# RWKV's chunked recurrence on TensorE: small products of one array shape in whole bursts, one PSUM bank for each chunk's output

## The chip, the cores and the metric

One core of one Trainium2 chip runs the whole program: TensorE (PE, with its weight loads as PEld), VectorE (DVE), ScalarE (ACT), GpSimd (POOL), SyncE (SP) and 16 DMA engines. The metric is the device time in microseconds of one execution, the median of several runs; lower is better.

## The reference

Two transformer blocks over 256 tokens of width 2048, all in float32. In the first, differential attention and an RWKV7 mixer work on the same normalised input, are gated, added and projected, and a feed-forward network follows. The second block holds stick-breaking attention, a state-space layer, sparse attention, cross attention and a convolutional feed-forward network; the change leaves it alone. What matters is the recurrence of RWKV7, 32 heads of 64 channels, one token at a time:

```
def _rwkv7_step(state, inp):
    r_t, w_t, k_t, v_t, a_t, b_t = inp
    sa = jnp.einsum('bhij,bhj->bhi', state, a_t)
    state = (state * w_t[:, :, None, :] + sa[..., None] * b_t[:, :, None, :]
             + v_t[..., None] * k_t[:, :, None, :])
    y = jnp.einsum('bhij,bhj->bhi', state, r_t)
    return state, y
```

## The kernel before, in words

**Weight products.** Most of the time goes to products with weights of 512 KB pieces. SP loads a piece, ScalarE rounds it to the high part WH (L163), VectorE subtracts to get the low part WL (L164), and TensorE multiplies three ways (L146 to L148, or in the transposed form L210, L211, L213). Such a product is a generator; each step issues a few matmuls and yields. A step is a tick.

**Lanes.** Everything else runs beside them as generators in lanes (`spawn`, `tick`), which yield the number of ticks to wait. While a lane must be finished before work can go on, `drain` ticks it and calls `fill`, which takes steps of weight products that are not urgent (the gate projections). The order of the emission gives each instruction a priority. A scheduler, working with its own estimate of times, then puts each engine's instructions into a fixed order: of those whose inputs it takes to be ready, the one emitted first. TensorE executes in that order, and a matmul that has to wait holds up all behind it.

**RWKV in chunks** (`rwkv`, L373). The 32 heads are four groups of eight: four tiles j of 128 channels, two heads o each on partition halves 0 to 63 and 64 to 127. The 256 tokens are four chunks c of 64. For each group:
- `rkv` (L469): the projections r, k, v of the group, 24 weight pieces;
- `rw_prep` (L505): decay factors, scaled operands AR and BK, in `s3` the bonus (L590) and the scores S (L597: for each half o, four chunks into one PSUM bank), transposed copies;
- `rw_chain` (L640): the inverse of a triangular 64x64 matrix of each head and chunk. VectorE inverts 32x32 diagonal blocks in 31 steps beside the next group's `rkv`; the results go through DRAM (dT, dX) to the tiles T1 and Xs. Two groups of 32x32 products (L701, L712) make the off-diagonal block, each evacuated by ScalarE in two halves (L705, L716);
- the recurrence itself (L721 to L766), chunk by chunk. Each chunk has five groups of 8 small matmuls, one for each (j, o): L727 (state into U, not in chunk 0), evacuated by two VectorE additions (L730); L736 (inverse times U), evacuated half by VectorE (L738), half by ScalarE (L739); L746 (next state, not in chunk 3), then L751 and L752 on VectorE; and for the output Y, in one loop over (j, o), L761 (state times AR, not in chunk 0) and L762 (UV times S) accumulate into the same piece of PSUM. L763 copies the output to Y. After most groups the generator yields 2 ticks;
- `rw_norm` (L768): group norm, bonus and gate, beside the preparation of the next group.

An f32 matmul shows up as two instructions in the trace. PSUM has eight banks of 512 f32 columns: four (`pm`) for weight products, four (`ps`) for all small products, taken and given back in turn.

The output loop before:

```
for j in range(4):
    for o in range(2):
        q = 64 * o
        out = ps[q:q + 64, j * 64:j * 64 + 64]
        if c:
            nc.tensor.matmul(out, St[q:q + 64, j], AR[q:q + 64, j, c, 1, :], start=True, stop=False)
        nc.tensor.matmul(out, UV[:, j, c, o], S[:, o, j, c, 64:128], start=(c == 0), stop=True)
```

Of the kernel before, what the change touches and what calls it, by code (L numbers as in the profile page):

```python
# [10 lines left out]
F32 = mybir.dt.float32  # L11
F32R = mybir.dt.float32r
AF = mybir.ActivationFunctionType
ALU = mybir.AluOpType
# [28 lines left out]
class K:  # L43
# [29 lines left out]
    # Side work runs in lanes: generators that yield the number of ticks to wait. A tick is one step of a  # L73
    # weight product (six matmuls), so that what a lane emits next on TensorE finds its operands ready.
# [83 lines left out]
    def split(self, w, p, WH, WL):  # L158
        """hi/lo of a pair of weight tiles"""
# [60 lines left out]
    def proj(self, w, nb, xa, dst, scale=1.0):  # L220
        """dst [128 channels, 4, T] = scale * (X @ W[:, 512 columns]).T"""
# [12 lines left out]
    def ln_exp(self):  # L234
        """loads the one table set that has both functions"""
        return self.nc.scalar.preload_act_table_set("natural_log_exp_and_others")

    def after(self, a, b):
        """a is scheduled after b"""
        self.tc.add_manual_dep(a.ins, b.ins.name, mybir.DependencyInfo(mybir.DependencyClass.NoSync, mybir.DependencyReason.DATA), reason="order")  # L240

    def to_hl(self, src, n, H, L, g=None, k0=0):
        """H/L[:, k0+kt, :] = hi/lo of (src(half, kt) transposed) * g[:, kt]."""
# [19 lines left out]
    def hl_both(self, pool, n=NKT):  # L263
        """room for a pair; hi and lo of a column tile are neighbours"""
# [6 lines left out]
    def rstd_of(self, ss, n, eps):  # L271
        """(ss / n + eps) ** -0.5 into a new [128, m] tile."""
# [6 lines left out]
    def rsqrt(self, r):  # L279
        """r <- r ** -0.5: a first guess from the exponent bits and three Newton steps"""  # L280
# [18 lines left out]
    # ---------------------------------------------------------------- program  # L299
# [35 lines left out]
    def x_in(self, xp):  # L335
        """the input, its transpose as hi/lo pair, and 1 / rms"""
# [168 lines left out]
    def rw_prep(self, g):  # L505
# [5 lines left out]
        # per-group LoRA weights  # L511
# [24 lines left out]
        # squared key norms (their maximum with the guard), inverted  # L536
# [20 lines left out]
            # a  # L557
# [5 lines left out]
            # k' = k * (1 + (a - 1) * k_a)  # L563
# [8 lines left out]
        def s2(j):  # L572
# [3 lines left out]
            # scaled operands  # L576
# [9 lines left out]
        def s3(j):  # L586
            # bonus
# [52 lines left out]
    def rw_chain(self, g):  # L640
        nc, rc, re = self.nc, self.rc, self.re
        AR, BKt, UV, S, G, bon, LB = self.rwg
        # inverses of the 32x32 diagonal blocks of I - A_ab (transposed), one block per partition
# [41 lines left out]
        for o in range(2):  # L685
            D_(T1[64 * o:64 * o + 32].rearrange("s j c t -> s (j c) t"), dT[o * 32:o * 32 + 16].rearrange("u s t -> s u t"))
# [7 lines left out]
        # off-diagonal block of the inverse  # L694
        Ms = re.tile([128, 16, 32], F32, tag="T1", name=self.nm("Ms"))
        ps = self.pst()
        for j in range(4):
            for c in range(4):
                for o in range(2):
                    q, u = 64 * o, 4 * j + c  # L700
                    nc.tensor.matmul(ps[q + 32:q + 64, u * 32:u * 32 + 32], S[q:q + 32, o, j, c, 32:64], T1[q:q + 32, j, c],  # L701
                                     start=True, stop=True, tile_position=(q, q + 32))
        for o in range(2):
            q = 64 * o
            nc.scalar.activation(Ms[q + 32:q + 64], ps[q + 32:q + 64].rearrange("p (u t) -> p u t", u=16), AF.Copy)  # L705
        yield 2
        ps = self.pst()
        for j in range(4):
            for c in range(4):
                for o in range(2):  # L710
                    q, u = 64 * o, 4 * j + c
                    nc.tensor.matmul(ps[q:q + 32, u * 32:u * 32 + 32], Ms[q + 32:q + 64, u], Xs[q + 32:q + 64, j, c, 32:64],  # L712
                                     start=True, stop=True, tile_position=(q + 32, q))
        for o in range(2):
            q = 64 * o
            nc.scalar.activation(Xs[q:q + 32, :, :, 32:64], ps[q:q + 32].rearrange("p (j c t) -> p j c t", j=4, c=4), AF.Copy)  # L716
# [3 lines left out]
        St = None  # L720
        for c in range(4):  # L721
            if c:
                ps = self.pst()
                for j in range(4):
                    for o in range(2):
                        q = 64 * o
                        nc.tensor.matmul(ps[q:q + 64, j * 64:j * 64 + 64], AR[q:q + 64, j, c, 0, :], St[q:q + 64, j], start=True, stop=True)  # L727
                for o in range(2):
                    u = UV[64 * o:64 * o + 64, :, c, o, :]
                    nc.vector.tensor_tensor(u, ps[64 * o:64 * o + 64, :256].rearrange("p (j t) -> p j t", j=4), u, op=ALU.add)  # L730
                yield 2
            ps = self.pst()
            for j in range(4):
                for o in range(2):
                    q = 64 * o
                    nc.tensor.matmul(ps[q:q + 64, j * 64:j * 64 + 64], Xs[q:q + 64, j, c], UV[q:q + 64, j, c, o], start=True, stop=True)  # L736
            pu = ps[:, :256].rearrange("p (j t) -> p j t", j=4)
            nc.vector.tensor_copy(UV[0:64, :, c, 0, :], pu[0:64])  # L738
            nc.scalar.activation(UV[64:128, :, c, 1, :], pu[64:128], AF.Copy)  # L739
            yield 2  # L740
            if c < 3:
                ps = self.pst()
                for j in range(4):
                    for o in range(2):
                        q = 64 * o
                        nc.tensor.matmul(ps[q:q + 64, j * 64:j * 64 + 64], BKt[:, j, c, q:q + 64], UV[:, j, c, o], start=True, stop=True)  # L746
# [3 lines left out]
                if c:  # L750
                    nc.vector.tensor_tensor(Sn, pn, St, op=ALU.add)  # L751
                    nc.vector.tensor_tensor(Sn, Sn, gb, op=ALU.mult)  # L752
                else:
                    nc.vector.tensor_tensor(Sn, pn, gb, op=ALU.mult)
            ps = self.pst()
            for j in range(4):
# [1556 lines left out]
```

## Time and profile before

| | |
|---|---|
| median of 3 runs | 3492.47 us (3492.26 to 3493.1) |
| span of the profiled execution | 3503.7 us |
| TensorE busy | 3365.8 us, 96% of the span |
| weight loads busy | 2784.5 us, 79% |
| VectorE, ScalarE, GpSimd busy | 2273.7, 1710.8, 684.8 us |
| RWKV stage, preparation of group 0 to recurrence of group 3 | about 130 to 795 us of the span |

The profile comes from an execution of its own; for it only the span is known. Times in the rows are from the start of that span. Busy time of TensorE counts an instruction from its start to its modelled end, so instructions overlap and a sum of durations is more than the time that passes; distances between starts are the safer measure. PEclk is the granted clock as a share of 2.4 GHz; it has two levels, 1.0 and 0.5, and a stretch shows the mean.

### The profile page before, as it was taken

The page shows a single profiled execution, that of the slowest core. Times are in us where ns is not written, and L with a number is a line of the kernel's source. Part 1 is how long each engine was busy: PE and PEld are TensorE (multiplying, and loading weights), DVE is VectorE, ACT ScalarE, POOL GpSimd, SP SyncE. Part 2 cuts the span into 40 slices and gives each one's busy share as a digit, 9 for nine tenths or more (in the row PEclk, how much of TensorE's full clock was granted, in tenths as well). Part 3 has the DMA queues.
Part 4 walks back from the last instruction along what each step waited for, and adds up shares of the span by engine and source line. Part 5 has one row for each costly group of instructions (what it writes and reads, how often), then busy time and mean ns, then how long its engine had stood idle before and what let it go on. Part 6 is the DMA issues. An engine that isn't in the chain of part 4 may idle for free.

```text
span 3503.7 us, 50392 instructions
## 1 busy us (share of the span) xinstructions
PE 3365.8 (96%) x18954; PEld 2784.5 (79%) x18954; DVE 2273.7 (65%) x3636; ACT 1710.8 (49%) x2675; POOL 684.8 (20%) x882
## 2 busy tenths in 40 slices
PE   8999999999999999999999999779999999999998
PEld 7877777778788888888888887557677788888886
DVE  5676675755766766554555565986777766566566
ACT  5544453534445555444443444336545554455453
POOL 0203021321211210210110101950103311011011
PEclk9999998989999999999999999979999999999999
DMA  6553534446656774666666665335456466666665
GB/s 213 154 169 98 150 107 126 127 137 190 202 180 185 263 246 151 189 187 192 186 187 193 187 202 186 115 106 175 135 169 203 144 188 188 191 187 189 190 186 156
DMA packets 177765, 607.04 MB, mean 173 GB/s; under 512 B 22427, under 2 KB 27372, under 8 KB 176752
## 3 DMA queue, kind: packets, MB, share of 16 engines
q1 hardware_dynamic: 168800, 580.25, 53.8%
q0 software_dynamic: 7856, 21.94, 2.0%
q8 instruction: 149, 2.44, 0.3%
q10 hardware_dynamic: 864, 1.62, 0.1%
q14 instruction: 96, 0.79, 0.1%
HBM read 584.29 MB, written 22.59 MB: 173 GB/s over the span
## 4 chain that ended last, share of the span: by engine, by line
PE 75%; DVE 8%; issue 6%; DMA 4%; ACT 2%; POOL 1%; DVEq 0%; ACTq 0%; POOLq 0%; SPq 0%
PE pm L211 26%; PE pm L210 12%; PE pm L146 9%; PE pm L147 9%; PE pm L148 9%; DVE WL L164 2%; PE ps L65 1%; PE ps L762 1%; ACT WH L163 1%; DVE s5x L1578 1%; PE ps L761 1%; PE pm L213 1%; DVE s5t L1578 1%; DMA T<-dT 1%; PE ps L1557 0%
## 5 line engine op out<-in xcount | busy, mean ns | idle before, releaser
L164 DVE TENSOR_TENSOR WL<-W,WH 128x1024 fp32r<-128x1024 f32 (+2 forms) x1016 | 1268.2, 1249 | 889.1 <-ACT WH L163 883.9
L211 PE MATMUL pm<-HL,WH 128*128 128x512 f32 x4928 | 1748.1, 401 | 9.1 <-ACT WH L163 4.4
L163 ACT ACTIVATE WH<-W 128x1024 fp32r<-128x1024 f32 (+2 forms) x1016 | 1066.7, 1050 | 1059.1 <-PE pm L148 446.8
L210 PE MATMUL pm<-HL,WL 128*128 128x256 f32 x4620 | 1317.0, 285 | 9.1 <-DVE WL L164 6.6
L211 PEld LDWEIGHTS pm<-HL,WH 128*128 128x128 f32 x4928 | 913.8, 189 | 212.2 <-DVE pt L492 7.6
L210 PEld LDWEIGHTS pm<-HL,WL 128*128 128x128 f32 x4620 | 876.1, 190 | 37.5 <-DVE WL L164 11.1
L147 PE MATMUL pm<-WL,HL 128*128 128x512 f32 (+1 forms) x1472 | 580.8, 395 | 16.7 <-DVE WL L164 16.7
L146 PE MATMUL pm<-WH,HL 128*128 128x512 f32 (+1 forms) x1472 | 587.3, 400 | 1.6 <-ACT WH L163 1.6
L148 PE MATMUL pm<-WH,HL 128*128 128x512 f32 (+1 forms) x1472 | 578.6, 393 | 0.7 <-DVE HL L1082 0.7
L147 PEld LDWEIGHTS pm<-WL,HL 128*128 128x128 f32 x1472 | 279.4, 190 | 78.4 <-DVE WL L164 22.7
L146 PEld LDWEIGHTS pm<-WH,HL 128*128 128x128 f32 x1472 | 278.5, 190 | 60.7 <-ACT WH L163 2.5
L148 PEld LDWEIGHTS pm<-WH,HL 128*128 128x128 f32 x1472 | 279.1, 190 | 59.1 <-DVE HL L1082 1.1
L2107 POOL TENSOR_TENSOR fcv<-fcv,fcv 128x256 f32<-128x256 f32 x44 | 51.8, 1177 | 544.2 <-DVE fcv L2094 535.1
L1140 POOL TENSOR_TENSOR sg<-sg,spr 128x256 f32<-128x256 f32 x44 | 45.6, 1053 | 389.9 <-ACT sg L1139 389.9
L213 PE MATMUL pm<-HL,WL 128*128 128x256 f32 x308 | 86.4, 281 | 0.2 <-DVE WL L164 0.2
L1149 POOL TENSOR_TENSOR HL<-fu,HL 128x256 fp32r<-128x256 f32 x44 | 48.3, 1119 | 195.2 <-ACT HL L1148 195.2
L1578 POOL TENSOR_TENSOR s5t<-s5x,PW 128x112 f32<-128x112 f32 (+3 forms) x136 | 73.3, 559 | 60.8 <-ACT s5x L1560 60.8
L2093 DVE SCALAR_TENSOR_TENSOR fcv<-fu,cw,fcv 128x255 f32<-128x255 f32 x88 | 54.3, 618 | 32.4 <-ACT fcv L2092 32.4
L2092 ACT ACTIVATE fcv<-fu,cw 128x256 f32<-128x256 f32 x88 | 52.4, 596 | 40.7 <-DVE fu L2091 40.7
L213 PEld LDWEIGHTS pm<-HL,WL 128*128 128x128 f32 x308 | 58.2, 189 | 12.7 <-DVE WL L164 0.9
L1578 DVE TENSOR_TENSOR s5x<-s5x,s5t 128x144 f32<-128x144 f32 (+3 forms) x140 | 67.0, 478 | 1.5
L1578 POOL TENSOR_TENSOR s5x<-s5x,s5t 128x112 f32<-128x112 f32 (+3 forms) x136 | 66.6, 513 | 0.2
(504 smaller groups left out, 3330.5 us busy)
## 6 DMA issues: line engine op xcount, KB each, us to landing
W<-in_w_ffi SPq DMA_DIRECT2D x176, 512.0 KB, 3.6
W<-in_w_up SPq DMA_DIRECT2D x176, 512.0 KB, 4.2
W<-in_w_rkv SPq DMA_DIRECT2D x96, 512.0 KB, 3.6
W<-in_w_qkv SPq DMA_DIRECT2D x96, 512.0 KB, 3.8
W<-in_w_ffo SPq DMA_DIRECT2D x88, 512.0 KB, 3.7
W<-in_w_down SPq DMA_DIRECT2D x88, 512.0 KB, 4.3
W<-in_w_gate SPq DMA_DIRECT2D x64, 512.0 KB, 3.7
W<-in_w_out SPq DMA_DIRECT2D x64, 512.0 KB, 4.3
```

The lines of the kernel that those rows point to most:

```text
L146: nc.tensor.matmul(o, a, WH[:, j], start=(k == 0), stop=False)
L147: nc.tensor.matmul(o, a, WL[:, j], start=False, stop=False)
L148: nc.tensor.matmul(o, b, WH[:, j], start=False, stop=(k == kts - 1))
L163: self.nc.scalar.activation(WH, W, AF.Copy)
L164: self.gated(self.nc.vector.tensor_tensor(WL, W, WH.bitcast(F32), op=ALU.subtract))
L210: nc.tensor.matmul(o[:, 0, ts], WL[:, kk, c], x[:, 0, ts], start=False, stop=False)
L211: nc.tensor.matmul(o[:, :, ts], WH[:, kk, c], x[:, :, ts], start=(k == 0), stop=(k == 15))
L213: nc.tensor.matmul(o[:, 0, ts], WL[:, kk, c], x[:, 0, ts], start=False, stop=False)
L1578: E.tensor_tensor(o, a, b, op=op)
L2092: nc.scalar.activation(c, u, AF.Identity, scale=cw[:, 2, ct:ct + 1], bias=cw[:, 3, ct:ct + 1])
L2093: nc.vector.scalar_tensor_tensor(c[:, 1:], u[:, 0:255], cw[:, 1, ct:ct + 1], c[:, 1:], op0=ALU.mult, op1=ALU.add)
L2107: nc.gpsimd.tensor_tensor(c, c, gs[i], op=ALU.mult)
```

## The change

Three places of the RWKV mixer. `s3` takes both PSUM banks of the scores first and issues the products with the halves o in alternation. In `rw_chain`, `burst` makes the first matmul of a group of small products wait for the last operation that its group needs, so that the group is whole once it starts. And the output of a chunk has a bank `psy` of its own from the beginning of the chunk: the state's part (L761) is issued right behind L727, the other part (L762) right behind L746, each as one run of 8 matmuls; since several accumulations are then open in one bank, only the first matmul of each partition half has the start flag. Comments are taken out elsewhere, which changes no instruction. Cut to its core:

```diff
+    def burst(self, mms, b):
+        self.tc.add_manual_dep(mms[0].ins, b.ins.name, mybir.DependencyInfo(mybir.DependencyClass.Sync, mybir.DependencyReason.DATA), reason="burst")
...
+            pss = [self.pst() for o in range(2)]
+            for c in range(4):
+                for o in range(2):
+                    pp = slice(64 * o, 64 * o + 64)
+                    nc.tensor.matmul(pss[o][:, c * 128:c * 128 + 128], BK[pp, c].rearrange("p a b -> p (a b)"),
+                                     AR[pp, j, c].rearrange("p a b -> p (a b)"), start=True, stop=True)
             for o in range(2):
-                pp = slice(64 * o, 64 * o + 64)
-                ps = self.pst()
-                for c in range(4):
-                    nc.tensor.matmul(ps[:, c * 128:c * 128 + 128], BK[pp, c].rearrange("p a b -> p (a b)"),
-                                     AR[pp, j, c].rearrange("p a b -> p (a b)"), start=True, stop=True)
-                nc.vector.tensor_tensor(S[:, o, j], ps.rearrange("p (c t) -> p c t", c=4),
+                nc.vector.tensor_tensor(S[:, o, j], pss[o].rearrange("p (c t) -> p c t", c=4),
                                         self.c("mask")[:, None, :].to_broadcast([128, 4, 128]), op=ALU.mult)
...
+        self.burst(mms, dT1)
...
+        self.burst(mms, last)
...
         for c in range(4):
+            psy = self.pst()
+            out = lambda j, o: psy[64 * o:64 * o + 64, j * 64:j * 64 + 64]
             if c:
                 ps = self.pst()
+                mms = []
+                for j, o in JO:
+                    q = 64 * o
+                    mms.append(nc.tensor.matmul(ps[q:q + 64, j * 64:j * 64 + 64], AR[q:q + 64, j, c, 0, :], St[q:q + 64, j], start=True, stop=True))
+                self.burst(mms, last)
+                for j, o in JO:
+                    q = 64 * o
+                    nc.tensor.matmul(out(j, o), St[q:q + 64, j], AR[q:q + 64, j, c, 1, :], start=(j == 0), stop=False, skip_group_check=True)
...
+                mms.append(nc.tensor.matmul(ps[q:q + 64, j * 64:j * 64 + 64], Xs[q:q + 64, j, c], UV[q:q + 64, j, c, o], start=True, stop=True))
+            self.burst(mms, last)
...
+            last = [nc.vector.tensor_copy(UV[0:64, :, c, 0, :], pu[0:64]), nc.scalar.activation(UV[64:128, :, c, 1, :], pu[64:128], AF.Copy)]
             yield 2
+            mms = []
             if c < 3:
                 ps = self.pst()
+                for j, o in JO:
+                    q = 64 * o
+                    mms.append(nc.tensor.matmul(ps[q:q + 64, j * 64:j * 64 + 64], BKt[:, j, c, q:q + 64], UV[:, j, c, o], start=True, stop=True))
+            for j, o in JO:
+                mms.append(nc.tensor.matmul(out(j, o), UV[:, j, c, o], S[:, o, j, c, 64:128], start=(c == 0 and j == 0), stop=(j == 3), skip_group_check=True))
+            for x in last:
+                self.burst(mms, x)
+                self.burst(mms[-8:], x)
...
-            ps = self.pst()
-            for j in range(4):
-                for o in range(2):
-                    q = 64 * o
-                    out = ps[q:q + 64, j * 64:j * 64 + 64]
-                    if c:
-                        nc.tensor.matmul(out, St[q:q + 64, j], AR[q:q + 64, j, c, 1, :], start=True, stop=False)
-                    nc.tensor.matmul(out, UV[:, j, c, o], S[:, o, j, c, 64:128], start=(c == 0), stop=True)
-            nc.scalar.activation(Y[:, :, c * 64:c * 64 + 64], ps[:, :256].rearrange("p (j t) -> p j t", j=4), AF.Copy)
+            nc.scalar.activation(Y[:, :, c * 64:c * 64 + 64], psy[:, :256].rearrange("p (j t) -> p j t", j=4), AF.Copy)
```

JO is the list of all (j, o), o running fastest. dT1 is the second of the two transfers from dT to T1; `last` is each time the operation that evacuated the group before.

## Rows read from the trace of the kernel before

**Rows 1.** Stage windows: us; PE, PEld, DVE, ACT, POOL; PEclk; DMA; GB/s.

```profile
243.00:295.00 52.00, 50.75 (x518) 36.89 (x519) 20.40 (x35) 17.25 (x34) 8.31 (x13) 0.97 0.23 69
295.00:330.00 35.00, 32.17 (x229) 26.78 (x230) 27.61 (x53) 21.93 (x42) 20.98 (x29) 1.00 0.33 99
400.00:460.00 60.00, 59.16 (x523) 41.33 (x523) 21.80 (x38) 17.35 (x33) 9.37 (x15) 0.83 0.19 59
568.00:630.00 62.00, 61.16 (x526) 42.90 (x525) 22.11 (x40) 18.77 (x36) 8.96 (x14) 0.81 0.15 45
735.00:795.00 60.00, 59.84 (x503) 43.89 (x504) 16.08 (x25) 14.49 (x24) 5.88 (x9) 0.77 0.28 87
```

**Rows 2.** TensorE's groups by line: shapes, count, busy us, mean ns.

```profile
L762 PE MATMUL ps<-S,UV 128*64 128x64 f32 x256 | 39.4, 260 | 0.0
L761 PE MATMUL ps<-AR,St 64*64 64x64 f32 x192 | 34.7, 267 | 0.0
L727 PE MATMUL ps<-St,AR 64*64 64x64 f32 x192 | 9.6, 250 | 0.0
```

**Rows 3.** TensorE's timeline, recurrence of group 0: start us, us, instructions.

```profile
264.85 0.33 PE L761 MATMUL ps<-AR,St 64*64 64x64 f32 x2
265.10 0.33 PE L762 MATMUL ps<-S,UV 128*64 128x64 f32 x2
...
267.41 0.32 PE L761 MATMUL ps<-AR,St 64*64 64x64 f32 x2
267.67 0.33 PE L762 MATMUL ps<-S,UV 128*64 128x64 f32 x2
```

**Rows 4.** The same timeline, runs of one line in chunks 0 and 1.

```profile
256.55 0.64 PE L762 MATMUL ps<-S,UV 128*64 128x64 f32 x13
...
257.67 0.68 PE L727 MATMUL ps<-St,AR 64*64 64x64 f32 x16
```

**Rows 5.** TensorE's timeline, recurrence of group 3, at the lower clock.

```profile
769.11 0.47 PE L761 MATMUL ps<-AR,St 64*64 64x64 f32 x2
769.51 0.47 PE L762 MATMUL ps<-S,UV 128*64 128x64 f32 x2
```

**Rows 6.** Stage windows of 4 us in the recurrence of group 1.

```profile
427.00:431.00 4.00, 4.00 (x43) 2.97 (x42) 1.89 (x3) 0.20 (x1) 0.00 (x0) 1.00 0.42 121
431.00:435.00 4.00, 4.00 (x29) 3.03 (x29) 0.83 (x2) 0.38 (x1) 0.00 (x0) 0.58 0.05 14
```

**Rows 7.** TensorE's timeline, a group of L736 that goes out in two parts.

```profile
252.15 0.39 PE L211 MATMUL pm<-HL,WH 128*128 128x512 f32 x1
...
252.50 0.39 PE L211 MATMUL pm<-HL,WH 128*128 128x512 f32 x1
252.82 0.32 PE L736 MATMUL ps<-UV,Xs 64*64 64x64 f32 x2
...
253.30 0.39 PE L211 MATMUL pm<-HL,WH 128*128 128x512 f32 x1
```

**Rows 8.** TensorE's timeline in preparation: scores, and L667.

```profile
297.28 1.71 PE L597 MATMUL ps<-AR,BK 64*128 64x128 f32 x16
...
327.18 1.15 PE L667 MATMUL ps<-UV,S 64*64 64x64 f32 x32
```

**Rows 9.** Waits of TensorE, 130 to 840 us: total us, times, longest.

```profile
PE ps L701 <- DMA T<-dT: 10.9, 4, 3.9
PE ps L590 <- DVE ob L807: 3.2, 2, 1.7
PE ps L590 <- DVE bon L591: 2.5, 1, 2.5
```

**Rows 10.** TensorE's timeline, group 0: the two parts of L701.

```profile
243.40 0.24 PE L701 MATMUL ps<-T,S 32*32 32x32 f32 x2 [1.85 <-DMA T<-dT]
...
246.81 1.40 PE L701 MATMUL ps<-T,S 32*32 32x32 f32 x62
```

**Rows 11.** VectorE's timeline, group 0: the evacuation of L727.

```profile
258.54 0.86 DVE L730 TENSOR_TENSOR UV<-ps,UV 64x256 f32<-64x256 f32 x2
```

More of the change, by code (lines that the diff above doesn't have):

```diff
@@ L685, in rw_chain @@
         for o in range(2):
-            D_(T1[64 * o:64 * o + 32].rearrange("s j c t -> s (j c) t"), dT[o * 32:o * 32 + 16].rearrange("u s t -> s u t"))
+            dT1 = D_(T1[64 * o:64 * o + 32].rearrange("s j c t -> s (j c) t"), dT[o * 32:o * 32 + 16].rearrange("u s t -> s u t"))
         for b in (1, 0):
@@ L700, in rw_chain @@
                     q, u = 64 * o, 4 * j + c
-                    nc.tensor.matmul(ps[q + 32:q + 64, u * 32:u * 32 + 32], S[q:q + 32, o, j, c, 32:64], T1[q:q + 32, j, c],
-                                     start=True, stop=True, tile_position=(q, q + 32))
+                    mms.append(nc.tensor.matmul(ps[q + 32:q + 64, u * 32:u * 32 + 32], S[q:q + 32, o, j, c, 32:64], T1[q:q + 32, j, c],
+                                                start=True, stop=True, tile_position=(q, q + 32)))
+        self.burst(mms, dT1)
         for o in range(2):
             q = 64 * o
-            nc.scalar.activation(Ms[q + 32:q + 64], ps[q + 32:q + 64].rearrange("p (u t) -> p u t", u=16), AF.Copy)
+            last = nc.scalar.activation(Ms[q + 32:q + 64], ps[q + 32:q + 64].rearrange("p (u t) -> p u t", u=16), AF.Copy)
         yield 2
         ps = self.pst()
+        mms = []
         for j in range(4):
@@ L711, in rw_chain @@
                     q, u = 64 * o, 4 * j + c
-                    nc.tensor.matmul(ps[q:q + 32, u * 32:u * 32 + 32], Ms[q + 32:q + 64, u], Xs[q + 32:q + 64, j, c, 32:64],
-                                     start=True, stop=True, tile_position=(q + 32, q))
+                    mms.append(nc.tensor.matmul(ps[q:q + 32, u * 32:u * 32 + 32], Ms[q + 32:q + 64, u], Xs[q + 32:q + 64, j, c, 32:64],
+                                                start=True, stop=True, tile_position=(q + 32, q)))
+        self.burst(mms, last)
         for o in range(2):
             q = 64 * o
-            nc.scalar.activation(Xs[q:q + 32, :, :, 32:64], ps[q:q + 32].rearrange("p (j c t) -> p j c t", j=4, c=4), AF.Copy)
+            last = nc.scalar.activation(Xs[q:q + 32, :, :, 32:64], ps[q:q + 32].rearrange("p (j c t) -> p j c t", j=4, c=4), AF.Copy)
         yield 2
@@ L720, in rw_chain @@
         St = None
+        JO = [(j, o) for j in range(4) for o in range(2)]
         for c in range(4):
+            psy = self.pst()
+            out = lambda j, o: psy[64 * o:64 * o + 64, j * 64:j * 64 + 64]
             if c:
                 ps = self.pst()
-                for j in range(4):
-                    for o in range(2):
-                        q = 64 * o
-                        nc.tensor.matmul(ps[q:q + 64, j * 64:j * 64 + 64], AR[q:q + 64, j, c, 0, :], St[q:q + 64, j], start=True, stop=True)
+                mms = []
+                for j, o in JO:
[5 more added lines that the diff above has]
+                    nc.tensor.matmul(out(j, o), St[q:q + 64, j], AR[q:q + 64, j, c, 1, :], start=(j == 0), stop=False, skip_group_check=True)
@@ L728, in rw_chain @@
                 for o in range(2):
                     u = UV[64 * o:64 * o + 64, :, c, o, :]
-                    nc.vector.tensor_tensor(u, ps[64 * o:64 * o + 64, :256].rearrange("p (j t) -> p j t", j=4), u, op=ALU.add)
+                    last = nc.vector.tensor_tensor(u, ps[64 * o:64 * o + 64, :256].rearrange("p (j t) -> p j t", j=4), u, op=ALU.add)
                 yield 2
             ps = self.pst()
[L733 to L736, printed above, removed]
+            mms = []
@@ L737, in rw_chain @@
+            for j, o in JO:
+                q = 64 * o
+                mms.append(nc.tensor.matmul(ps[q:q + 64, j * 64:j * 64 + 64], Xs[q:q + 64, j, c], UV[q:q + 64, j, c, o], start=True, stop=True))
+            self.burst(mms, last)
             pu = ps[:, :256].rearrange("p (j t) -> p j t", j=4)
-            nc.vector.tensor_copy(UV[0:64, :, c, 0, :], pu[0:64])
-            nc.scalar.activation(UV[64:128, :, c, 1, :], pu[64:128], AF.Copy)
+            last = [nc.vector.tensor_copy(UV[0:64, :, c, 0, :], pu[0:64]), nc.scalar.activation(UV[64:128, :, c, 1, :], pu[64:128], AF.Copy)]
@@ L740, in rw_chain @@
             yield 2
+            mms = []
             if c < 3:
                 ps = self.pst()
[L743 to L746, printed above, removed]
+                for j, o in JO:
+                    q = 64 * o
+                    mms.append(nc.tensor.matmul(ps[q:q + 64, j * 64:j * 64 + 64], BKt[:, j, c, q:q + 64], UV[:, j, c, o], start=True, stop=True))
@@ L747, in rw_chain @@
+            for j, o in JO:
+                mms.append(nc.tensor.matmul(out(j, o), UV[:, j, c, o], S[:, o, j, c, 64:128], start=(c == 0 and j == 0), stop=(j == 3), skip_group_check=True))
+            for x in last:
+                self.burst(mms, x)
+                self.burst(mms[-8:], x)
+            if c < 3:
                 pn = ps[:, :256].rearrange("p (j t) -> p j t", j=4)
@@ L751, in rw_chain @@
                     nc.vector.tensor_tensor(Sn, pn, St, op=ALU.add)
-                    nc.vector.tensor_tensor(Sn, Sn, gb, op=ALU.mult)
+                    last = nc.vector.tensor_tensor(Sn, Sn, gb, op=ALU.mult)
                 else:
-                    nc.vector.tensor_tensor(Sn, pn, gb, op=ALU.mult)
-            ps = self.pst()
-            for j in range(4):
-                for o in range(2):
-                    q = 64 * o
-                    out = ps[q:q + 64, j * 64:j * 64 + 64]
-                    if c:
-                        nc.tensor.matmul(out, St[q:q + 64, j], AR[q:q + 64, j, c, 1, :], start=True, stop=False)
-                    nc.tensor.matmul(out, UV[:, j, c, o], S[:, o, j, c, 64:128], start=(c == 0), stop=True)
-            nc.scalar.activation(Y[:, :, c * 64:c * 64 + 64], ps[:, :256].rearrange("p (j t) -> p j t", j=4), AF.Copy)
+                    last = nc.vector.tensor_tensor(Sn, pn, gb, op=ALU.mult)
+                St = Sn
+            nc.scalar.activation(Y[:, :, c * 64:c * 64 + 64], psy[:, :256].rearrange("p (j t) -> p j t", j=4), AF.Copy)
             if c < 3:
-                St = Sn
                 yield 2
```

## Prediction

> **What bounds the kernel now.** I read the stage windows first, because the change touches one stage: the four rounds of the RWKV recurrence. In the stretches that hold the recurrences TensorE is busy nearly all the time (50.75 of 52 us, 59.84 of 60 in the fourth), VectorE and ScalarE are busy less than half of it, and the DMA share is below 0.3 [rows 1]. So in these 234 us TensorE sets the pace, and since it is busy for 96% of the whole span, what it saves there brings everything behind it forward. The same rows show a second thing: the granted clock is 0.97 in the first stretch, but 0.83, 0.81 and 0.77 in the others, while it is 1.00 in the preparation that follows [rows 1].
>
> The second view groups TensorE's instructions by line. L761 and L762, the two products of a chunk's output, have the same tiny size as L727, but 192 of L761 keep the engine busy for 34.7 us and 256 of L762 for 39.4, against 9.6 us for 192 of L727 [rows 2]. The timeline says why. L761 and L762 are emitted alternately, two instructions (one f32 matmul) each, and every such pair starts 0.25 to 0.26 us after the one before [rows 3]. Emitted in a run, the same instructions cost far less: 13 of L762 take 0.64 us from first start to last end, 16 of L727 take 0.68 [rows 4], some 0.05 us for one, the time to drain included, instead of 0.13. L761 is 64x64, L762 128x64 (contraction by output columns) [rows 2]: what costs is the change of shape, not the work.
>
> **1. Alternation removed.** Twelve chunks (three of four, in four groups) alternate 8 + 8 matmuls: 192 pairs by 0.257 us are 49 us. About 47 of the pairs run at the half clock, 0.40 us apart [rows 5], which adds 47 x 0.146 = 7: 56 us. Afterwards L761 stands behind L727 (same shape) and L762 behind L746 (same shape): 12 runs of each, 16 instructions by 0.03 to 0.04 us [rows 4], 12 x (0.5 + 0.6) = 13 us. Gain 43. Bounds: 36, if all that was at half clock stays so and the new runs too are sometimes slow; 46, if a run costs 0.035 for one.
>
> **2. Clock.** By the clocks of [rows 1], time at the half level (1.2 GHz) is 2 x length x (1 - clock): 3, 20, 24 and 28 us, 75 in all; half of it, 37 us, is lost. The fall comes with the alternation: 427 to 431 us, with two alternating runs just behind it, is at 1.00, the next 4 us at 0.58 [rows 6]. In the first group, though, the same pattern keeps the clock. Its 3 us come from the wait for DMA in point 5; taken four times, that is 12 of the 75. The other 63 cost 31 us, of which 7 are in point 1, so at most 24 are left. I take two thirds, 16, since the low stretches become shorter and the weight products closer; bounds 0 and 24 as a gain (a loss is a rival, below).
>
> **3. Splits removed.** Where a group of small products waits for two evacuations, its first two instructions go out alone, weight products follow, and the rest comes later. Two starts of L211 are 0.35 us apart in a row of weight products and 0.80 with such an excursion between [rows 7]: 0.45, less 0.07 for the two instructions themselves. I count 30 in the timeline (8, 8, 8 and 6 in the four groups, on L701, L712, L736, L746): 11 us. The wait for the last evacuation now stands in front of the whole burst. Bounds 5 (the scheduler puts a ready weight product into the burst nonetheless) and 13.
>
> **4. Scores.** L597 issues all products of one partition half, then those of the other: 16 take 1.71 us. L667, which alternates halves, runs 32 in 1.15 [rows 8]; its moving side is half as long (64 columns for 128). Scaled, 16 of L597 in alternation take 0.5 to 0.9 us if halves overlap, 1.7 if not: 16 steps by 0.8, 13 us, or nothing. This is preparation, where TensorE is busy 32 of 35 us and waits for banks and operands (L590, 5.7 us in three waits) [rows 1, 9]; part of the gain will turn into such waits. I take 6. A rule speaks against this edit: the Trainium skill, TensorEngine Tiling (Array Packing), Restrictions and Gotchas, says that row tiles raise the pressure on PSUM, because different row tiles need different banks. No row before shows two row tiles at once; the rival below prices it.
>
> **5. Wait for T.** L701's first two instructions wait for T<-dT in each group, 10.9 us in all [rows 9]. After the wait in group 0 (1.85 us) weight products fill the 3.4 us until the other 62 start [rows 10]. With the whole burst tied to the second of the T transfers, those products can go ahead of the wait. Gain 5, bounds 0 (the second transfer lands later, and the engine comes earlier) and 11.
>
> **6. What is added.** A burst waits for both evacuations instead of one: behind it in TensorE's in-order queue stand the weight products, and behind those the evacuations to gate. A pair of L730 takes 0.86 us [rows 11]; L761 (0.5 us) now stands in that gap, and weight products as well, so I cost most of it at nothing; uncovered, 48 stages by 0.4 us are 19. PSUM: one of the four ps banks is held from L761 to the copy of Y; the chain alone needs two, so nothing until chunk 3, where the next preparation starts. I add 4; bounds 0 and 19. No DMA, no SP or POOL instruction moves; the stripped comments are no instructions.
>
> **A rule against point 1.** L746 and L762 use all 128 rows. In the rows, 13 of L762 in 0.64 us leave 0.05 for one, load included [rows 4]. The Trainium skill, TensorE: Matmul & The Clock Gate, Part 3, says that a weight load overlaps running matmuls only when the row group differs. By that rule, with its 64 columns at 1.2 GHz, an estimate of 0.05 us of load would be added to each L762, 12 x 16 x 0.05 = 10 us less gain; the trace disagrees, since the whole of load and product already fits in 0.05.
>
> **Sum.** -43 - 16 - 11 - 6 - 5 + 4 = -77 us. The profiled execution spans 3503.7 us, 11.2 above the median of 3492.47; the instructions last the same in both, so I take the 77 off the median: **3415 us**.
>
> **Rivals.**
> - *Latency takes over* (15%). With less TensorE work, chains of burst, evacuation, burst set the pace. For: preparation and the wait for T already show idle time [rows 1, 9]. Against: the shortest recurrence I can add up (15 stages of 0.6 us burst and about 0.6 us evacuation, 18 us, by [rows 4, 11]) is far below the 52 us of the first stretch, which holds little else. If half of points 1 to 3 turns into idle time: -77 + 35 = -42, **3450 us**.
> - *Banks in preparation* (8%). The two banks of the scores must be free at once, with a third for the bonus, out of four. L590 already waits up to 2.5 us for such evacuations [rows 9]. If 12 of the 16 steps wait 2 us more and point 4 gives nothing: -77 + 6 + 24, **3446 us**. This is the rule of the tiling page, working here through L590.
> - *The bursts do not stay whole, or the clock still falls* (12%): points 2 and 3 give nothing: **3442 us**.
> - *The clock stays low in all four recurrences* (3%, the slower side). Bursts are small products closer together, and TensorE does little work in them. The four stretches hold 234 - 37 = 197 us of work at full clock; less 36 and 11 that is 150. Wholly at half clock it is 300, 66 longer than now: with points 4 and 5, 55 slower, **3548 us**. It decides from 168 us at the half level (150 + 168/2 = 234), against 75 now. Against: group 0 runs all its alternations at 1.00, and the stretch just before the fall is at 1.00 as well [rows 6].
> - *Nothing moves* (2%): the scheduler's order was the limit and undoes the emission: 3492 us.
>
> **Numbers.** The forecast has 60%; its own range, from the bounds that are not extreme at once, is 3390 to 3440. The range for 8 in 10 must take in most of the first three rivals: 3388 to 3458. The measurement can tell 0.2%, 7 us, from no change. Slower by that: the clock rival and stray changes of the scheduler's order, 0.04; the same: 0.03; faster: 0.93.
>
> **What would show it.** Right: L761 and L762 in runs of 16 at about 0.04 us for one, their busy time near 10 and 15 us; no two-instruction excursions; clock above 0.9 in the recurrences; L597's 16 in about 0.9 us. Wrong: idle time of TensorE ahead of L736, L727 or L590 that grew by tens of us; the clock below 0.8; or a stretch after the RWKV stage that is longer by what was gained.

## The result and the profile after

The changed kernel takes 3434.1 us (median of 4 runs, 3423.45 to 3437.08) against 3492.36 for the kernel before (3487.2 to 3493.1): ratio 0.9839, interval 0.9813 to 0.9865. Measured once more beside the experiments it took 3422.17 us (3419.15 to 3434.07) against 3489.64, ratio 0.9811 (0.9786 to 0.9835). The gain is 58 us in the first of these measurements and 67 in the second. (The ratios here and below are not the quotients of the medians beside them.) Executions of the kernel before spread from 3474 to 3507 us over the three comparisons below, and by and large the longer ones are those with the lower mean granted clock (0.985 to 0.974).

The profiled execution took 3433.04 us, with a span of 3431.3 (3503.7 before). Stage windows show where the 72 us between the two spans went. The first fence is the kernel before, cut at the first product after the wait for T and at the first product of the norm: four recurrences, and the preparation that follows the first. The second is the changed kernel, cut at the same places, with four short windows around its last wait for T. Columns as in [rows 1].

```profile
243.40:288.80 45.40, 45.40 (x490) 32.68 (x491) 14.51 (x27) 12.75 (x23) 4.43 (x7) 0.96 0.25 75
288.80:399.80 111.00, 105.37 (x660) 88.53 (x658) 93.66 (x183) 63.30 (x106) 30.40 (x43) 1.00 0.51 152
399.80:452.40 52.60, 52.60 (x490) 36.05 (x491) 15.58 (x27) 12.89 (x25) 4.45 (x7) 0.81 0.21 67
...
565.80:620.80 55.00, 55.00 (x490) 38.22 (x491) 13.64 (x24) 12.73 (x23) 4.04 (x6) 0.76 0.17 54
...
735.20:794.60 59.40, 59.40 (x501) 43.53 (x502) 15.88 (x25) 14.38 (x23) 5.67 (x9) 0.77 0.28 86
```

```profile
244.80:277.20 32.40, 31.91 (x485) 24.45 (x486) 14.82 (x25) 13.77 (x24) 4.20 (x7) 0.95 0.35 110
277.20:396.30 119.10, 111.21 (x680) 92.38 (x681) 95.11 (x185) 63.38 (x106) 30.33 (x44) 0.97 0.50 146
396.30:428.50 32.20, 31.95 (x485) 24.52 (x486) 13.29 (x24) 12.61 (x23) 4.04 (x6) 0.95 0.28 95
...
545.60:576.00 30.40, 29.87 (x480) 22.75 (x481) 15.72 (x25) 13.77 (x26) 8.53 (x11) 1.00 0.40 123
...
688.20:723.50 35.30, 35.09 (x482) 27.32 (x483) 14.34 (x23) 13.33 (x22) 3.00 (x4) 0.92 0.29 95
...
684.00:688.20 4.20, 0.03 (x2) 0.06 (x3) 0.00 (x0) 0.00 (x0) 0.00 (x0) 0.50 1.04 319
688.20:692.00 3.80, 3.80 (x70) 3.54 (x71) 0.42 (x1) 1.50 (x3) 0.00 (x0) 0.50 0.41 109
692.00:696.00 4.00, 4.00 (x75) 3.17 (x75) 0.42 (x1) 1.96 (x5) 0.73 (x1) 0.78 0.01 4
696.00:700.00 4.00, 3.79 (x31) 2.58 (x30) 2.69 (x3) 2.95 (x5) 2.27 (x3) 1.00 0.25 87
```

The recurrences fall from 212.4 us to 130.3, by 82, at a granted clock of 0.92 to 1.00 instead of 0.76 to 0.96. The three stretches between them (norm of one group, preparation and inverse of the next) grow, from 111.0, 113.4 and 114.4 us to 119.1, 117.1 and 112.2: 10 back. Before the first recurrence and behind the last little moves (243.4 and 244.8 us; 2709.1 and 2707.8). What stands against each other in these 10 us: some 5 are weight products that no longer find room in the recurrences (31 instructions more than before, by 0.175 us, half of the 0.35 of [rows 7]), some 7 are clock (0.97, 0.99 and 0.98 in the three stretches, against 1.00), and 2.7 are idle time of TensorE (21.8 us before, 24.5 after); the scores, below, take less.

TensorE's groups by line of the changed kernel; L765 is the L762 of [rows 2], L744 the L761, L740 the L727:

```profile
L765 PE MATMUL ps<-S,UV 128*64 128x64 f32 x256 | 10.4, 224 | 0.0
L744 PE MATMUL ps<-AR,St 64*64 64x64 f32 x192 | 7.6, 218 | 0.0
L740 PE MATMUL ps<-St,AR 64*64 64x64 f32 x192 | 8.2, 224 | 0.0
```

Same instructions, same count: 39.4 us became 10.4, and 34.7 became 7.6. TensorE's timeline shows the whole bursts that answer to [rows 3, 4], then the scores that answer to [rows 8], once early and once behind a wait, then the wait for T in group 3 with weight products behind it:

```profile
252.46 0.68 PE L753 MATMUL ps<-UV,Xs 64*64 64x64 f32 x16
...
254.31 0.69 PE L763 MATMUL ps<-UV,BKt 128*64 128x64 f32 x16
254.83 0.64 PE L765 MATMUL ps<-S,UV 128*64 128x64 f32 x16
255.39 0.39 PE L210 MATMUL pm<-HL,WL 128*128 128x256 f32 x1
...
256.06 0.68 PE L740 MATMUL ps<-St,AR 64*64 64x64 f32 x16
256.57 0.63 PE L744 MATMUL ps<-AR,St 64*64 64x64 f32 x16
257.13 0.50 PE L211 MATMUL pm<-HL,WH 128*128 128x512 f32 x1
...
284.72 1.16 PE L601 MATMUL ps<-AR,BK 64*128 64x128 f32 x16
285.81 0.66 PE L65 MATMUL ps<-par,vT 128*128 128x128 f32 x4
...
311.93 1.22 PE L594 MATMUL ps<-pr,cst 128*128 128x256 f32 x2 [2.03 <-DVE S L604]
...
313.93 2.09 PE L601 MATMUL ps<-AR,BK 64*128 64x128 f32 x16
...
688.17 1.92 PE L707 MATMUL ps<-T,S 32*32 32x32 f32 x64 [6.47 <-DMA T<-dT]
...
690.40 0.63 PE L211 MATMUL pm<-HL,WH 128*128 128x512 f32 x1
...
691.04 0.63 PE L211 MATMUL pm<-HL,WH 128*128 128x512 f32 x1
```

A run of 16 takes 0.56 us to the next start (254.83 to 255.39, 256.57 to 257.13). The excursions of two instructions of [rows 7] are gone. Sixteen instructions of the scores take 1.09 us (284.72 to 285.81) instead of 1.64 in the kernel before, from 297.28 [rows 8] to the next start:

```profile
298.92 0.66 PE L65 MATMUL ps<-par,vT 128*128 128x128 f32 x4
```

That would be 16 x 0.55 = 9 us over all steps, but it is not what came. In the changed kernel 10 of the 16 steps take 1.09 to 1.16 us; two still go out in two parts of 8 (1.08 to 1.15 us for each part), the other four take 1.48 to 2.02 us, two of them at the lower clock. The scores' busy time went from 28.6 to 23.2 us: 5 us less on TensorE, not 9.

TensorE's waits, 130 to 800 us, of the changed kernel (total, times, longest), and the row for S of the kernel before:

```profile
PE ps L707 <- DMA T<-dT: 10.0, 4, 6.5
PE ps L594 <- DVE S L604: 4.4, 2, 2.4
PE ps L554 <- DVE S L604: 1.9, 2, 1.1
PE ps L65 <- DVE S L604: 1.7, 1, 1.7
PE ps L763 <- ACT UV L756: 0.7, 2, 0.5
```

```profile
PE ps L550 <- DVE S L599: 1.6, 2, 0.8
```

Against [rows 9], the wait for T barely moved (10.9 to 10.0). The waits for VectorE's evacuation of the scores S rose from 1.6 to 8.0 us, while those for the bonus and for `ob` became shorter; TensorE's whole idle time in the three stretches between the recurrences grew by only 2.7 us. Of the added waits of the bursts, one shows here with 0.7 us; in the four recurrences together TensorE is idle for 1.5 us, before for none.

### The profile page after: what moved, and what is told of

It reads as the page before. It is cut to its first block, busy times and chain, and to the rows that moved or that the text cites. A ratio compares the mean times of both kernels' runs of the same rounds, so it can differ in the third digit from the quotient of the medians.

```text
span 3431.3 us, 50392 instructions
## 1 busy us (share of the span) xinstructions
PE 3297.2 (96%) x18954; PEld 2743.5 (80%) x18954; DVE 2269.6 (66%) x3636; ACT 1710.4 (50%) x2675; POOL 686.9 (20%) x882
## 4 chain that ended last, share of the span: by engine, by line
PE 72%; DVE 8%; issue 8%; DMA 3%; ACT 2%; POOL 1%; DVEq 0%; POOLq 0%; ACTq 0%; SPq 0%
PE pm L211 25%; PE pm L210 12%; PE pm L146 9%; PE pm L147 9%; PE pm L148 9%; DVE WL L164 2%; PE ps L65 1%; DVE s5x L1593 1%; ACT WH L163 1%; PE pm L213 1%; DMA T<-dT 1%; DVE s5t L1593 1%; PE ps L1572 0%; DMA dT<-TM 0%; PE ps L1854 0%
## 5 line engine op out<-in xcount | busy, mean ns | idle before, releaser
L210 PEld LDWEIGHTS pm<-HL,WL 128*128 128x128 f32 x4620 | 875.3, 189 | 35.7 <-DVE WL L164 10.4
```

The lines of the kernel that those rows point to most:

```text
L210: nc.tensor.matmul(o[:, 0, ts], WL[:, kk, c], x[:, 0, ts], start=False, stop=False)
```

## The experiments

Each comparison has its own runs of the kernel before. The clock differs from run to run, so the table also gives an estimate: time times mean granted clock of each run, the median of these, which is the time if all had run at the upper level. It takes time at the lower level as half lost; two weight products take 0.64 us there (690.40 to 691.04 above) and 0.35 at the upper [rows 7], so it overstates the clock's share a little.

| kernel | median us (n) | ratio, 95% | clock | estimate |
|---|---|---|---|---|
| before, first comparison | 3488.94 (19) | | 0.978 | 3417 |
| e1_output_runs_only | 3442.68 (4) | 0.9872 [0.9838, 0.9907] | 0.985 | 3389 |
| e2_burst_waits_only | 3478.87 (10) | 0.9964 [0.9940, 0.9988] | 0.980 | 3411 |
| e3_scores_only | 3490.52 (10) | 1.0006 [0.9982, 1.0030] | 0.979 | 3418 |
| e4_old_scores | 3424.83 (4) | 0.9830 [0.9798, 0.9862] | 0.986 | 3377 |
| before, second | 3486.55 (7) | | 0.980 | 3416 |
| e5_alternate_other_piece | 3459.16 (4) | 0.9911 [0.9877, 0.9944] | 0.983 | 3400 |
| e6_mix_same_shape | 3420.63 (4) | 0.9802 [0.9771, 0.9834] | 0.986 | 3372 |
| before, third | 3489.64 (11) | | 0.979 | 3417 |
| e7_changed_again | 3422.17 (5) | 0.9811 [0.9786, 0.9835] | 0.985 | 3371 |
| e8_old_scores_again | 3421.85 (6) | 0.9807 [0.9781, 0.9834] | 0.986 | 3376 |
| e9_bonus_last | 3418.00 (5) | 0.9800 [0.9774, 0.9826] | 0.986 | 3370 |

### One part at a time

**Runs alone.** The changed kernel with the old order of the scores and without the added waits; only the output's runs and their bank are left.

```diff
     def burst(self, mms, b):
-        self.tc.add_manual_dep(mms[0].ins, b.ins.name, mybir.DependencyInfo(mybir.DependencyClass.Sync, mybir.DependencyReason.DATA), reason="burst")
+        return
...
-            pss = [self.pst() for o in range(2)]
-            for c in range(4):
-                for o in range(2):
+            for o in range(2):
+                ps = self.pst()
+                for c in range(4):
```

> Only the output of a chunk is changed: a bank of its own, the state's part behind the products of L727, the other part behind those of L746. No burst waits, scores as before. Theory (a change of shape from one matmul to the next costs, and the clock falls behind the alternation): most of the gain is here, 45 to 65 us below the kernel before; the output's two lines busy for 18 us together instead of 74; some 30 two-instruction excursions stay; clock at 0.9 or more in the recurrences. Rival (the gain comes from the bursts being whole, which keeps the clock up): below 30 us, clock near 0.8 in the recurrences of groups 1 to 3.

It gained 46 us. The group of L762 is busy for 15.5 us, that of L761 for 7.6: 23 together, where 18 were expected. The recurrences stand at a clock of 1.00, 1.00, 0.79 and 0.94, so the 0.9 that was expected was missed in group 2.

**Waits alone.** The kernel before with `burst` on L701, L712, L727, L736, L746 and on the output loop, whose alternation stays.

```diff
+                self.burst(mms, last)
...
+            for x in prev:
+                self.burst(mms, x)
```

> Only the burst waits are added; the output's two products alternate as before and the scores are as before. Theory: the excursions go, 5 to 15 us gained; the output's two lines stay at 70 us or more of busy time together, and the clock in the recurrences of groups 1 to 3 stays near 0.8. Rival (whole bursts keep the clock up): 30 us or more gained, clock above 0.9 although the shapes alternate.

It gained 10 us (6 by the estimate), and the two lines of the output are still busy for 34.5 and 31.6 us, 66 together. The clock was not near 0.8 as expected: 0.92, 0.89, 0.89 and 0.89 in the four recurrences. So whole bursts, in this one profile, do part of what the rival said, though the gain is far from its 30 us.

**Scores alone.** The kernel before with the new loop of `s3`.

```diff
-            for o in range(2):
-                ps = self.pst()
-                for c in range(4):
+            pss = [self.pst() for o in range(2)]
+            for c in range(4):
+                for o in range(2):
```

> Only the scores are changed (halves in alternation, two banks at once); the recurrence is as before. Theory: 16 of the scores' instructions take 1.1 us instead of 1.64, 9 us over all steps, of which some 5 arrive: time 0 to 8 us lower. Rival (banks in preparation): TensorE's waits for the evacuation of the scores (VectorE) grow by as much or more, from the end of norm to the end of preparation no stretch is shorter, time 0 to 10 us higher.

Nothing that can be told from noise: ratio 1.0006, interval 0.9982 to 1.0030, some 8 us to either side. The scores' busy time fell from 28.6 us to 24.0, so 5 us and not the 9 that were expected.

**All but the scores**, measured twice, the second time beside the changed kernel itself; the diff is the last one, reversed, on the changed kernel.

> The changed kernel with the scores as before. Theory: 3 to 8 us slower than the changed kernel. Rival (banks in preparation): equal or up to 10 us faster than the changed kernel, with preparation (first group norm product to the wait for T) shorter by 2 to 4 us in each group and no wait of TensorE on the scores' evacuation above 1 us.

> The changed kernel once more, beside the next two, with more runs. Theory and rival alike: 45 to 70 us below the kernel before, as measured.

> The changed kernel with the scores as before, once more, to tell it from the changed kernel. Theory now (banks in preparation: what the alternating scores save is lost in waits for their two banks): 3 to 12 us faster than the changed kernel. Rival (the difference seen first was chance): within 3 us of it or slower.

In the third comparison, side by side with the changed kernel, it takes 3421.85 us against 3422.17. Both theories missed: it was neither slower, as the first said, nor faster, as the second said. The scores' edit is worth nothing that these comparisons can measure, with or without the other parts; 5 us are within their noise.

Since the clock differs between executions, the parts are best compared in recurrences that ran wholly at the upper level. One row each, group 1: the scores-alone kernel (the old recurrence), the runs-alone kernel (with four windows from its group 2, for later), and the changed kernel measured again.

```profile
399.70:442.40 42.70, 42.69 (x483) 30.69 (x484) 13.60 (x25) 12.70 (x23) 4.43 (x7) 1.00 0.24 77
```

```profile
389.70:424.70 35.00, 34.96 (x488) 25.64 (x488) 14.59 (x25) 12.75 (x24) 4.18 (x7) 1.00 0.34 105
...
540.40:545.00 4.60, 4.58 (x74) 3.85 (x75) 0.42 (x1) 0.52 (x2) 1.06 (x2) 0.62 0.55 186
545.00:550.00 5.00, 5.00 (x72) 3.80 (x73) 1.01 (x2) 3.15 (x6) 0.73 (x1) 0.50 0.02 3
550.00:555.00 5.00, 5.00 (x26) 3.48 (x27) 0.86 (x2) 1.30 (x3) 1.55 (x2) 0.50 0.56 157
555.00:560.00 5.00, 5.00 (x69) 4.10 (x71) 0.91 (x3) 1.49 (x3) 0.00 (x0) 0.64 0.00 0
```

```profile
393.30:424.40 31.10, 30.75 (x486) 23.48 (x487) 13.34 (x24) 12.66 (x23) 4.04 (x6) 1.00 0.32 100
```

42.7 to 35.0 to 31.1. The runs save 7.7 us, 8.6 when the five weight products more that this stretch holds are counted (0.175 each). The waits save 3.9, or 3.5 for the two products fewer. Over four groups that is 34 and 14 us.

### Is it the shape, or the sum on the piece just written?

In the kernel before, L762 not only has another shape than L761 but also adds to the piece of PSUM that L761 has just written. The next kernel alternates the shapes again, shifted by two, so that no matmul adds to the piece of the one ahead of it. The one after issues two lines and two banks matmul by matmul, but of one shape.

```diff
-                for j, o in JO:
-                    q = 64 * o
-                    nc.tensor.matmul(out(j, o), St[q:q + 64, j], AR[q:q + 64, j, c, 1, :], start=(j == 0), stop=False, skip_group_check=True)
...
+            for i in range(10 if c else 8):
+                if c and i < 8:
+                    j, o = JO[i]
+                    q = 64 * o
+                    mms.append(nc.tensor.matmul(out(j, o), St[q:q + 64, j], AR[q:q + 64, j, c, 1, :], start=(j == 0), stop=False, skip_group_check=True))
+                i -= 2 if c else 0
+                if i >= 0:
+                    j, o = JO[i]
+                    mms.append(nc.tensor.matmul(out(j, o), UV[:, j, c, o], S[:, o, j, c, 64:128], start=(c == 0 and j == 0), stop=(j == 3), skip_group_check=True))
```

> The changed kernel, but the state's part of the output is taken back to the other part and the two alternate again, shifted by two: a matmul of the second part never adds to the piece of PSUM that was written just before. Theory (the change of shape costs): a pair of instructions takes 0.25 to 0.26 us again, 3.4 us for a chunk instead of 1.2, 27 us over the twelve chunks, and the clock falls somewhat oftener: 25 to 50 us slower than the changed kernel. Rival (a matmul that adds to the piece written just before waits for it): runs at 0.04 us for one instruction, within 10 us of the changed kernel.

Its timeline of TensorE, chunk 1 of group 0:

```profile
261.39 0.33 PE L770 MATMUL ps<-S,UV 128*64 128x64 f32 x2
261.64 0.33 PE L766 MATMUL ps<-AR,St 64*64 64x64 f32 x2
261.90 0.33 PE L770 MATMUL ps<-S,UV 128*64 128x64 f32 x2
262.16 0.32 PE L766 MATMUL ps<-AR,St 64*64 64x64 f32 x2
```

Every pair again starts 0.25 to 0.26 us after the one ahead, as in [rows 3], though it adds to another piece. It takes 39 us more than the next kernel, measured in the same comparison; part of that is clock (0.983 against 0.986), and 28 are left by the estimate, against the 27 of the working.

```diff
                     mms.append(nc.tensor.matmul(ps[q:q + 64, j * 64:j * 64 + 64], AR[q:q + 64, j, c, 0, :], St[q:q + 64, j], start=True, stop=True))
-                self.burst(mms, last)
-                for j, o in JO:
-                    q = 64 * o
                     nc.tensor.matmul(out(j, o), St[q:q + 64, j], AR[q:q + 64, j, c, 1, :], start=(j == 0), stop=False, skip_group_check=True)
+                self.burst(mms, last)
```

(L763 and L765 are mixed in the same way.)

> The changed kernel, but within each burst the two products of the same shape alternate matmul by matmul: L740 with L744 (64x64), L763 with L765 (128x64); so the PSUM bank changes with each matmul, the shape does not. Theory (only the change of shape costs): 32 instructions take 1.1 to 1.3 us as in the changed kernel, time within 10 us of it. Rival (what costs is changing bank and line from matmul to matmul): a pair takes 0.15 us or more, 30 us or more slower than the changed kernel.

Its timeline, chunk 1 of group 0:

```profile
255.15 0.34 PE L740 MATMUL ps<-St,AR 64*64 64x64 f32 x4
255.32 0.29 PE L741 MATMUL ps<-AR,St 64*64 64x64 f32 x4
255.43 0.33 PE L740 MATMUL ps<-St,AR 64*64 64x64 f32 x4
255.55 0.33 PE L741 MATMUL ps<-AR,St 64*64 64x64 f32 x4
```

Four instructions (two matmuls, one on each partition half) take 0.12 us, although the line and the bank change after each four: 0.03 for one, as in a run. The changed kernel's ratio is 0.9811, this one's 0.9802, the shifted alternation's 0.9911. So it is the change of shape that costs; the sum on the piece just written, the bank and the line do not. Shown is that for this pair of shapes, 64x64 and 128x64; no run tries another.

### The third bank in preparation

The scores now hold two of the four small banks while the bonus (L594) holds a third. If that is what eats the scores' gain, moving the bonus behind them should give it back.

```diff
-            ps = self.pst()
-            nc.tensor.matmul(ps[:, :256], self.c("bones"), pr, start=True, stop=True)
-            nc.vector.tensor_tensor(bon[:, j, :], ps[:, :256], vT[:, j, 64:320], op=ALU.mult)
             pss = [self.pst() for o in range(2)]
...
+            ps = self.pst()
+            nc.tensor.matmul(ps[:, :256], self.c("bones"), pr, start=True, stop=True)
+            nc.vector.tensor_tensor(bon[:, j, :], ps[:, :256], vT[:, j, 64:320], op=ALU.mult)
```

> The changed kernel with the bonus product emitted behind the scores instead of ahead of them, so that the scores need two free banks and not a third for the bonus at the same time. Theory (banks in preparation): TensorE's waits on the evacuation of the scores (8 us in the changed kernel) shrink to below 4, 3 to 8 us faster than the changed kernel. Rival (the waits are VectorE's, which has too much to do in preparation): waits move to other lines, within 3 us of it.

It takes 3418.00 us against 3422.17; the intervals of the two ratios overlap. Its waits of TensorE, 130 to 800 us:

```profile
PE ps L819 <- DVE bon L604: 3.4, 4, 1.1
PE ps L563 <- DVE bon L604: 3.2, 1, 3.2
PE ps L65 <- DVE ob L821: 3.1, 2, 1.6
PE ps L554 <- DVE S L600: 2.5, 2, 1.3
```

The waits for S are smaller (4.0 us in all, with 1.5 at L65), and waits for the bonus and for `ob` stand in their place. The four shown end on VectorE. Over the three stretches between the recurrences TensorE is idle for 23.7 us, in the changed kernel for 24.5 and 25.6 (its two profiles): giving back a bank early for the most part only changes the matmul that waits.

This is the lowest median of all, but not told apart from the changed kernel, and neither are e6 and e8. No version that was tried clearly beats the changed kernel.

## Why the prediction was right, and where it was off

**Direction and mechanism: right.** 3415 us was forecast, 3422 and 3434 were measured. The time came out of the recurrences, through the lines and by the mechanism that [rows 2 to 4] pointed to. Points 1 to 3 carry it; points 4 and 5 brought next to nothing.

**Point 1, alternation: right.** 43 us were expected, 36 of them at the upper clock level. The rows at that level give 34, and the runs alone gave 46 with their share of the clock. The 12 runs of each line cost 0.56 us, as costed. On the rule weighed against this point (the Trainium skill, TensorE: Matmul & The Clock Gate, Part 3: a load overlaps only where the row group differs), the trace of the changed kernel disagrees again: 16 instructions of L765, all on 128 rows, start and make room for the next in 0.56 us, 0.035 for one, load included.

**Point 2, clock: the size came out, the cause is shown in part.** In the recurrences, 2 x length x (1 - clock) gives 77 us at the lower level before, and 3.2 + 3.2 + 0 + 5.6 = 12 us after: the 12 that were left to the waits for T. The last four windows of the changed kernel above show where those lie: around the wait for T of group 3, TensorE stands idle, works some 6 us at 1.2 GHz (clock 0.50), and is then back at 2.4 (1.00). The fall of [rows 6], which comes in the middle of a recurrence while TensorE is busy all the time, is in no profile of the changed kernel. Nor is it in that of the runs alone, but there a low stretch that began at the wait for T in group 2 lasted over 15 us of the recurrence (its last four windows above). With the waits but the old alternation (e2) falls in the middle are there and short, the recurrences at 0.89 to 0.92. With the shifted alternation and whole bursts (e5) only group 3 has one, and groups 0 to 2 stand at 0.96, 1.00 and 0.96:

```profile
734.00:738.00 4.00, 4.00 (x45) 2.88 (x43) 1.85 (x3) 0.14 (x1) 0.00 (x0) 1.00 0.38 134
738.00:742.00 4.00, 4.00 (x32) 2.84 (x32) 0.84 (x2) 0.39 (x1) 0.00 (x0) 0.57 0.00 1
```

In the RWKV stage, falls under load are in all four profiles with alternation (before, e2, e3, e5) and in none of the seven without it (after, e1, e4, e6 to e9), which bears out that the fall comes with the alternation. But alternation does not bring it every time (group 1 of e3 ran at 1.00), and with split bursts there was most of it. There is one profile of each kernel, two of the changed one, and what exactly lets the clock fall stays open; the two thirds of point 2 were a guess that came out. By the estimates of the table, 46 of the 67 us (3417 to 3371) are work and waits and the other 21 are clock, against the 16 of this point and the 7 in point 1.

**Point 3, splits: right.** 11 us expected; the waits alone gave 10 (6 by the estimate), and behind the runs the rows at the upper level give 14 with what belongs to point 5.

**Point 4, scores: wrong.** Sixteen instructions with the halves in alternation take 1.09 us instead of 1.64. By the Trainium skill, TensorEngine Tiling (Array Packing), Overview, a short dimension of 64 or less gains up to 2 times; here it was 1.5 against the old order, and 2.0 against two halves one by one (1.08 us each, where the scores go out in two parts). The step that failed first is the 0.8 us for a step. Its scaling left out the wider moving side: L667 runs 16 in half of 1.15 us, and scaled by the columns, of which the scores have twice as many, that is 1.15, not 0.5 to 0.9. And the old order was not without overlap: both halves together took 1.64, not 2.16. So a whole step saves 0.55, and as not every step runs so, all of them save 5 us, where 13 were worked out. The second step, "part of the gain will turn into such waits", is not settled. The waits for S rose from 1.6 to 8.0 us. The Trainium skill, TensorEngine Tiling (Array Packing), Restrictions and Gotchas, says that row tiling raises the pressure on PSUM; these waits agree with it. But TensorE's whole idle time between the recurrences is the same with the old order of the scores (24.6 and 25.1 us in e4 and e8) as with the new (24.5 and 25.6), so the waits for S mostly stand where others stood. By the estimate of the table the new order is worth 5 us (3376 to 3371), which a lower clock would have taken back, but the runs of the two overlap in it, and the scores alone (e3) show no such gain. Where the 5 us stay is open. The rival in the prediction, which lost 24 us to the banks, was far too dear. That a wait can cost clock had no term: behind 2.03 us of wait for S, the changed kernel's scores at 313.93 took 2.09 us instead of 1.16, at the lower level (0.50 from 312 to 316).

**Point 5, T: wrong.** 5 us were taken, 1 came at the wait itself (10.9 to 10.0). The step that failed is "those products can go ahead of the wait": in the order that the scheduler made they still stand behind the burst (690.40 in group 3 above), and TensorE is busy for only 0.03 us of the last 4.2 of a wait of 6.47. Why they were not put ahead is not shown. That the transfer lands no earlier while TensorE comes earlier, the reason given for the lower bound, would fit the longer wait in group 3 (6.5 us, before at most 3.9), but no run tests it.

**Point 6, added waits: too dear.** 4 us were taken; TensorE's idle time in the recurrences rose from 0 to 1.5 us, 0.7 of it at L763. The cover named for it (L744 and weight products in the gap) held.

**The sum.** With points 4 and 5 at 0 and 1, and point 6 at 1: -43 - 16 - 11 - 1 + 1 = -70, against 67 measured in the third comparison and 58 in the first. "The instructions last the same in both" was wrong, and that may be part of what is left: the span stood 11 us above the median at a clock of 0.977, where the runs of the third comparison have 0.979 at their median, which is some 7 us. The profile of e3 (0.979) has 56 us at the lower level in the same old recurrences, not 77. So part of point 2 was not there to be won in a median run. The 10 us given back in preparation, moved weight products among them, had no term either; "a stretch after the RWKV stage that is longer by what was gained" was looked for, but it is the stretch between the recurrences that grew.

## What to carry to other kernels

Small products are emitted in runs of one array shape. Where data flow leaves a choice, order by shape: two small matmuls of different shapes (here 64x64 and 128x64) next to each other cost 0.25 us for each at the full clock, in a run 0.07. A saving of a few us in a stage that also has waits may not show in the time: the scores' 5 us of TensorE did not, so measure such a part by itself before it is counted. And where the granted clock differs between executions of one kernel, a gain read from a single profile is measured from that execution, not from the median.

## What was not expected of the hardware

- Changing the bank and the line among small matmuls of one shape costs nothing: 4 instructions in 0.12 us, mixed or not. Changing the shape between 64x64 and 128x64 costs: the start of each pair moves from about 0.06 or 0.07 us to 0.255 behind the one ahead.
- With the new order, the lower clock level in the RWKV stage stands only behind idle time of TensorE, for 3 to 10 us each time in the two profiles of the changed kernel. In the old order it also came under full load and stayed for up to 20 us (from 432 to 452 in group 1).
